# Two-block transformer on one core: the recurrence's order table without zero products, and four steps on other engines

## The chip, the core and the metric

The program runs on one core of a Trainium2 chip. TensorE multiplies matrices, VectorE and GpSimd do elementwise work from and to SBUF (VectorE reads PSUM as well), ScalarE applies activations and scaled copies, SyncE issues the DMAs here. Each engine works through its own list of instructions in order, and waits at semaphores for the others. In the profile's rows they are PE (PEld for the weight loads), DVE, POOL, ACT and SP. The metric is the device time of one execution in microseconds; smaller is better.

## The reference, cut to what matters

The model has a first block (convolution, attention with forgetting, a gated feed-forward) and a second block of two layers, of which the first is a recurrence over 528 positions in 32 heads of 64. Only the recurrence is touched:

```python
kk = (k * k_k); kk = kk / max(norm(kk), 1e-12)         # per head
k = k * (1 + (a - 1) * k_a)
decay = exp(-exp(w))
a_vec, b_vec = -kk, kk * a
def step(S, inp):                                      # S: 64x64 per head
    sa = einsum('bhij,bhj->bhi', S, a_t)
    S = S * w_t + sa * b_t + v_t * k_t
    return S, einsum('bhij,bhj->bhi', S, r_t)
y = (y - mean(y)) * rsqrt(var(y) + GN_EPS)             # per head
y = (y * ln_w + ln_b + bonus) * silu(g)
return y @ w_out
```

## The kernel before

The recurrence is computed in chunks: one of 16 positions and eight of 64. Two heads that fill 128 partitions make a pair, so there are 16 pairs (class `Pair`). For a pair the steps that don't depend on the state are written as generators, cut into pieces by `yield`: `rates` (letter F, decays), `keys` (K, a projection of 48 products of 128x128 by 128x264), `operands` (O), `blocks` (B, small triangular inverses of 16x16, 14 pairs of small products and sums on GpSimd in a row), `inverse` (L) and `merge` (X, the inverses put together to 64x64), `mats` (M, transposes), `weights` (P), `post` (Q, the norm over a head and the gate). `chain` is the recurrence itself: per chunk three steps, each a few small products on TensorE and a move of their result out of PSUM that the next step needs (Z and U on ScalarE, the state S on VectorE).

There is no scheduler: the order of the instructions on every engine is the order in which the code is run. A round starts a new pair's chain (15 of its 27 steps, N) and ends the old pair's (12 steps, O); `MAIN` says in which order the two take turns, and `PLAN` has a word for each of the 27 turns, whose letters say which pieces follow it. A piece that yields 1 leaves its second half (the move out of PSUM) to the next turn or piece. In the same round run the pieces of later pairs: K and F three pairs ahead, O, B and V two ahead, M, X and L one ahead, Q two behind. Rounds -1 to 12 have them all; in the last three the projections and operands have run out and the output projection's pieces stand at K.

The letter D is `fill` (L2175 to 2181): two products with a weight of zeros that add nothing to the sum that `keys` has open. They carry no result. The table has 11 of them in a round.

The names to follow, in the order of `operands`: `sq` (L2032, ScalarE, from `kx`), `kp2` (L2034), `kk` (ScalarE), `n2` (L2043, sums of squares on TensorE), the norms `nv` (L2049, L2050), `mi` (L2055, a mask times the norms), `al` (L2060), `rho` (L2063), `bd` (L2067, L2068, first operands for chunk 0, four small products), `kk2` (L2071), `be` (L2077 and for chunk 0 L2078: beta into `fix_kb`), `ka` (L2080, L2081: kappa into `fix_kb`), then the products `n00` to `n11` (L2101) of `fix_kb` with `AR`, and `n_first` (L2109). The norms' order matters: `kk2` overwrites what `bd` reads. From `n11` and `n_first` the matrix goes to DRAM and back into `n16`, from which `blocks` starts (L2149); at its end it is written out and a transposed copy `t16` of it made (L2158). In `post` the last steps are y (L2389) and the gate (L2391). Which engine does a step says the table `ENG`: a for ScalarE, d for VectorE, p for GpSimd.

Of the kernel before, what the change touches and what calls it, by code (L numbers as in the profile page):

```python
# [1802 lines left out]

PLAN = ("OMOO", "OMOOOKMMD", "OOD", "MLD", "KMQQD", "OPOD", "KPOQKD", "OPOOXQO", "QOKMOKQ", "", "XXKO", "OKQ", "QXKQK", "BXQKK", "MXBQX", "O", "BOMBBXX", "KKQXD", "KBBBD", "BKFD", "XFOQVKFQXQD", "KFQXD", "BXKXFKKK", "FQ", "BMFOKBKQ", "RBBFMB", "KKOXBXKB")

ENG = dict(kx="d", kp2="p", bd="d", ld="p", wc="d", kp="d", kk="a", mi="d", al="d", rho="p", be="d", ka="p", KT="a", vt0="a", vt1="a", KT0="a", VU0="a", y2="a", r2="d", U="a", y0="d", yt="d", no0="p", no1="a", y="d", sg="d", t16="d", Z="a", sc="d", rk="p", kk2="d")  # L1810


def both(new, old):

    for x in MAIN:
        g = new if x == "N" else old
# [3 lines left out]

MAIN = "NONONONONNONONONONNONONONON"


def weave(main, streams):
# [4 lines left out]
    def flush():  # L1831
        while held:
            pull(held.pop())
# [7 lines left out]

    for (i, _), step in zip(enumerate(main), PLAN):
        flush()
# [30 lines left out]
class Pair:  # L1874
# [39 lines left out]
    def ev(s, key, out, x, scale=None, bias=None):  # L1914

        e = ENG[key]
        if e == "a":
# [11 lines left out]
    def en(s, key):  # L1929
        return s.nc.vector if ENG[key] == "d" else s.nc.gpsimd  # L1930

# [94 lines left out]
    def operands(s):  # L2026
# [42 lines left out]
        yield  # L2069
        if ENG["kk2"] == "d":  # L2070
            nc.vector.scalar_tensor_tensor(kk, ta, 1.0, kk, ALU.add, ALU.mult)  # L2071
# [11 lines left out]
        s.rk = T_("rk")  # L2083
        if ENG["rk"] == "d":
            nc.vector.scalar_tensor_tensor(s.rk, rP, k.v("r_k", p), kp, ALU.mult, ALU.mult)
# [198 lines left out]
    def chain(s):  # L2284
# [5 lines left out]
        for c in range(NC_):  # L2290
# [23 lines left out]
            for h, q in enumerate(HS):  # L2314
                mm(z[u, P + 64 * h:P + 64 * h + 64], lhsT=R[u, hw[h]], rhs=Z[u, q], start=h == 0, stop=h == 1)  # L2315
            if ENG["U"] == "d":
                h2 = lambda a: a.rearrange("p (h t) -> p h t", h=2)
# [107 lines left out]
```

## Time and profile before

| | us |
|---|---|
| median of 3 runs (2447.52 to 2453.63) | 2450.68 |
| the profiled execution | 2448.32 |
| its span, first to last instruction | 2446.5 |
| PE busy | 2282.0 (93%) |
| PE weight loads busy | 1964.4 (80%) |
| DVE busy | 1317.8 (54%) |
| POOL busy | 1234.6 (50%) |
| ACT busy | 1001.8 (41%) |

The page of the profile says of busy PE that matmuls are pipelined and their ends modelled: a matmul's row runs from its start to its modelled end, and the next starts before that. How long a product holds TensorE up is read from the start of one row to the start of the next. The idle time that a row shows in brackets is time in which the engine had nothing running, and what ended it; a wait that fits under the tail of the product before is not shown as idle. The recurrence's rounds with all streams lie between 1130 and 1663 us of the span.

### The profile page before, as it was taken

To read this page: it belongs to the slowest core of one execution; us is meant where nothing else is said; L and a number is where in the kernel's file an instruction comes from. 1 tells how busy PE (TensorE), PEld (TensorE's weight loads), DVE (VectorE), ACT (ScalarE), POOL (GpSimd) and SP (SyncE) were. 2 spreads that over 40 slices of the span, in tenths; PEclk is the share of its full clock that TensorE was granted. 3 is DMA by queue.
4 is the path that set the end of the run, shared out by engine and by line. 5 is a ranking of instruction groups with operands and counts; after the bars stand their busy time and mean duration, and the time that the engine had idled before them with its cause. 6 is when DMAs were issued, how large, how long until landed. Compare 5 with 4: busy or idle time off the path is not lost. (4 is left out here: it accounts for less than half of the span.)

```text
span 2446.5 us, 42606 instructions
## 1 busy us (share of the span) xinstructions
PE 2282.0 (93%) x16754; PEld 1964.4 (80%) x16754; DVE 1317.8 (54%) x2860; ACT 1001.8 (41%) x2292; POOL 1234.6 (50%) x1414
## 2 busy tenths in 40 slices
PE   7999999999998999888999999999977898899996
PEld 5788888878887999877888888887877777887885
DVE  6662135734756450323676767676334633765665
ACT  5553333423434442323354444544332422554442
POOL 5235455656655654535456565655333644344433
PEclk9999999999998999998999999997988899999998
DMA  3113222222232423332222323223223332112212
GB/s 130 69 70 122 104 86 87 98 83 104 98 100 86 172 99 126 102 104 85 70 61 55 80 65 74 70 59 103 67 77 110 126 106 101 59 61 64 66 53 96
DMA packets 135496, 217.05 MB, mean 89 GB/s; under 512 B 60864, under 2 KB 85888, under 8 KB 125056
## 3 DMA queue, kind: packets, MB, share of 16 engines
q1 hardware_dynamic: 123168, 191.63, 24.8%
q10 hardware_dynamic: 12128, 22.70, 2.5%
q8 instruction: 132, 2.16, 0.4%
q14 instruction: 68, 0.56, 0.1%
HBM read 179.28 MB, written 35.00 MB: 88 GB/s over the span
## 5 line engine op out<-in xcount | busy, mean ns | idle before, releaser
L261 POOL TENSOR_TENSOR wlo<-wraw,whi 128x512 fp32r<-128x512 f32 (+1 forms) x312 | 440.2, 1440 | 332.8 <-ACT whi L260 332.7
L941 POOL TENSOR_TENSOR wlo<-wraw,whi 128x512 fp32r<-128x512 f32 (+2 forms) x207 | 255.1, 1246 | 320.4 <-ACT whi L940 312.8
L260 ACT ACTIVATE whi<-wraw 128x512 fp32r<-128x512 f32 (+1 forms) x312 | 175.3, 615 | 252.7 <-issue 73.7
L940 ACT ACTIVATE whi<-wraw 128x512 fp32r<-128x512 f32 (+2 forms) x207 | 115.2, 590 | 55.7 <-PE p_o_t L1715 19.4
L269 PE MATMUL pu<-f_xh,whi 128*128 128x512 f32 x336 | 131.2, 391 | 0.0
L271 PE MATMUL pu<-f_xh,wlo 128*128 128x512 f32 x336 | 130.8, 389 | 0.0
L270 PE MATMUL pu<-f_xl,whi 128*128 128x512 f32 x336 | 130.8, 389 | 0.0
L2321 ACT ACTIVATE VU<-z,fix_nv 64x64 f32<-64x64 f32 x256 | 63.2, 301 | 147.0 <-PE z L2315 146.6
L2331 DVE SCALAR_TENSOR_TENSOR fix_S<-fix_S,wc,z 64x64 f32<-64x64 f32 x224 | 62.4, 278 | 93.2 <-PE z L2327 50.2
L1305 POOL COPY ap<-apr 128x96 f32<-128x96 f32 x64 | 16.9, 264 | 141.6 <-DVE apr L1302 102.0
L2154 POOL TENSOR_TENSOR r<-r,t 66x14 f32<-66x14 f32 (+6 forms) x224 | 77.9, 348 | 17.5
L2015 PE MATMUL pk<-lh_k,whi 128*128 128x264 f32 x256 | 81.8, 320 | 1.6 <-DVE kx L1923 1.6
L2015 PE MATMUL pk<-lh_k,wlo 128*128 128x264 f32 x256 | 82.3, 322 | 0.0
L2015 PE MATMUL pk<-ll_k,whi 128*128 128x264 f32 x256 | 79.5, 311 | 0.0
L1601 PE MATMUL p_g<-lh_g,wlo 128*128 128x264 f32 x256 | 73.7, 288 | 2.7 <-POOL wlo L941 2.5
L2152 POOL TENSOR_TENSOR t<-n,r 66x14 f32<-66x14 f32 (+6 forms) x224 | 66.9, 299 | 16.2
L1601 PE MATMUL p_g<-lh_g,whi 128*128 128x264 f32 x256 | 74.8, 292 | 0.0
L269 PEld LDWEIGHTS pu<-f_xh,whi 128*128 128x128 f32 x336 | 63.1, 188 | 13.4 <-issue 0.2
L816 DVE SCALAR_TENSOR_TENSOR ab<-z,vecs,ab 128x511 f32<-128x511 f32 x44 | 55.6, 1265 | 33.7 <-ACT ab L815 33.7
L271 PEld LDWEIGHTS pu<-f_xh,wlo 128*128 128x128 f32 x336 | 63.1, 188 | 13.1
L270 PEld LDWEIGHTS pu<-f_xl,whi 128*128 128x128 f32 x336 | 63.1, 188 | 13.1 <-issue 0.2
L1601 PE MATMUL p_g<-ll_g,whi 128*128 128x264 f32 x256 | 73.1, 286 | 0.0
(850 smaller groups left out, 7508.1 us busy)
## 6 DMA issues: line engine op xcount, KB each, us to landing
wraw<-in_w_up_dram SPq DMA_DIRECT2D x22, 1024.0 KB
wraw<-in_w_dn_dram SPq DMA_DIRECT2D x16, 704.0 KB
wraw<-in_a_h_dram SPq DMA_DIRECT2D x16, 640.0 KB
wraw<-in_l_k_dram SPq DMA_DIRECT2D x16, 576.0 KB
wraw<-in_w_gt_dram SPq DMA_DIRECT2D x8, 1024.0 KB
wraw<-in_l_v_dram SPq DMA_DIRECT2D x8, 1024.0 KB
wraw<-in_l_r_dram SPq DMA_DIRECT2D x8, 1024.0 KB
wraw<-in_l_g_dram SPq DMA_DIRECT2D x16, 512.0 KB
```

The source lines that it names most:

```text
L260: nc.scalar.activation(hi[:p, o], raw[:p, o], AF.Copy)
L261: nc.gpsimd.tensor_tensor(lo[:p, o], raw[:p, o], hi[:p, o].bitcast(F32), ALU.subtract)
L269: nc.tensor.matmul(out, lhsT=wh, rhs=xh, start=start and k == 0, stop=False)
L270: nc.tensor.matmul(out, lhsT=wh, rhs=xl, start=False, stop=False)
L271: nc.tensor.matmul(out, lhsT=wl, rhs=xh, start=False, stop=stop and k == n - 1)
L940: nc.scalar.activation(hi[:, o], raw[:, o], AF.Copy)
L941: nc.gpsimd.tensor_tensor(lo[:, o], raw[:, o], hi[:, o].bitcast(F32), ALU.subtract)
L1601: nc.tensor.matmul(b[:, :HL], lhsT=a, rhs=c[:, o], start=kk == 0 and n == 0, stop=kk == KB - 1 and n == 2)
L2015: s.nc.tensor.matmul(b_[:, :HL], lhsT=a, rhs=b[:, o], start=i == 0 and q == 0, stop=last)
L2152: g.tensor_tensor(tmp[:, :q, :m], n16[:, :q, q:q + 1].to_broadcast([66, q, m]), r16[:, q:q + 1, q + 1:].to_broadcast([66, q, m]), ALU.mult)
L2154: g.tensor_tensor(r16[:, :q, q + 1:], r16[:, :q, q + 1:], tmp[:, :q, :m], ALU.add)
L2321: nc.scalar.activation(VU[u, q], z[u, P + 64 * h:P + 64 * h + 64], AF.Copy, scale=s.nv[u, nv + h:nv + h + 1])
```

## The change

A new `PLAN` and a new `MAIN`. The new table has the same number of letters O, K, B, F, X, Q, P, L, V and R, no D, and two M more (which come after the stream's end and do nothing). In `ENG` four entries change: `bd` and `be` go from VectorE to GpSimd, `y` from VectorE to GpSimd, `t16` from VectorE to ScalarE.

```diff
-PLAN = ("OMOO", "OMOOOKMMD", "OOD", "MLD", "KMQQD", "OPOD", "KPOQKD", "OPOOXQO", "QOKMOKQ", "", "XXKO", "OKQ", "QXKQK", "BXQKK", "MXBQX", "O", "BOMBBXX", "KKQXD", "KBBBD", "BKFD", "XFOQVKFQXQD", "KFQXD", "BXKXFKKK", "FQ", "BMFOKBKQ", "RBBFMB", "KKOXBXKB")
+PLAN = ("OMOO", "OOKMM", "OOOOM", "", "KMLQ", "OQOPOK", "KPM", "QOPOXQ", "QOOKMOKQ", "", "MXXBQKOO", "O", "KKQXQK", "QKKXB", "XBQXM", "", "MXOBKB", "QKXXXK", "MBBB", "BQBFQ", "XFOOBKVKFQX", "FQ", "RKFKQKK", "OF", "BKXKXBK", "FBKKMF", "XXBBOKMBQ")
...
-ENG = dict(kx="d", kp2="p", bd="d", ld="p", wc="d", kp="d", kk="a", mi="d", al="d", rho="p", be="d", ka="p", KT="a", vt0="a", vt1="a", KT0="a", VU0="a", y2="a", r2="d", U="a", y0="d", yt="d", no0="p", no1="a", y="d", sg="d", t16="d", Z="a", sc="d", rk="p", kk2="d")
+ENG = dict(kx="d", kp2="p", bd="p", ld="p", wc="d", kp="d", kk="a", mi="d", al="d", rho="p", be="p", ka="p", KT="a", vt0="a", vt1="a", KT0="a", VU0="a", y2="a", r2="d", U="a", y0="d", yt="d", no0="p", no1="a", y="p", sg="d", t16="a", Z="a", sc="d", rk="p", kk2="d")
...
-MAIN = "NONONONONNONONONONNONONONON"
+MAIN = "NONONONONNONONONONONNONONON"
```

Three places show what moves; all are of round 5, in which chain 5 begins and chain 4 ends. A name's second number is the pair.

TensorE ahead of the operands' products, from the last products of chunk 5 of pair 4's chain on (`pk0_8` is the projection for pair 8). Before:

```order
L2324 MATMUL z5_4_12520<-VU_4_11351,AYb_4_10927 64x64 [waits Activation_49]
L2324 MATMUL z5_4_12520<-VU_4_11351,AYb_4_10927 64x64
L2327 MATMUL z5_4_12520<-VU_4_11351,KTb_4_11350 64x64 x2
L2180 MATMUL pk0_8_12554<-lh_k_7906,fix_zero_7996 128x264 x2
L2306 MATMUL z1_5_12639<-fix_S2_7971,AR_5_11389 128x128 [waits DVE_49]
L2308 MATMUL z1_5_12639<-VU_5_11931,AN_5_11387 64x64 x2
L2015 MATMUL pk0_8_12554<-ll_k_7907,whi108_12052 128x264
L2015 MATMUL pk0_8_12554<-lh_k_7906,wlo108_12053 128x264
L2015 MATMUL pk0_8_12554<-lh_k_7906,whi108_12052 128x264
L2015 MATMUL pk0_8_12554<-ll_k_7907,whi108_12052 128x264
L2180 MATMUL pk0_8_12554<-lh_k_7906,fix_zero_7996 128x264 x2
L2306 MATMUL z6_4_12659<-fix_S1_7970,AR_4_10809 128x128 [waits DVE_49]
```

The same place now, with the first of the operands' products at its end:

```order
L2324 MATMUL z5_4_12388<-VU_4_11263,AYb_4_10849 64x64
L2327 MATMUL z5_4_12388<-VU_4_11263,KTb_4_11262 64x64 x2
L2015 MATMUL pk0_8_12412<-ll_k_7907,whi108_11936 128x264
L2015 MATMUL pk0_8_12412<-lh_k_7906,wlo108_11937 128x264
L2306 MATMUL z1_5_12502<-fix_S2_7971,AR_5_11316 128x128 [waits DVE_49]
L2308 MATMUL z1_5_12502<-VU_5_11821,AN_5_11293 64x64 x2
L2015 MATMUL pk0_8_12412<-lh_k_7906,whi108_11936 128x264
L2015 MATMUL pk0_8_12412<-ll_k_7907,whi108_11936 128x264
L2306 MATMUL z6_4_12513<-fix_S1_7970,AR_4_10758 128x128 [waits DVE_49]
L2308 MATMUL z6_4_12513<-VU_4_11263,AN_4_10735 64x64 x2
L2101 MATMUL n00_7_12524<-AR_7_12432,fix_kb0_7981 128x128 [waits Activation_49,Pool_49]
```

The zero products between the chains' steps are gone, and fewer real ones stand in their place: two between z1 and z6 where four and two zeros stood.

ScalarE at the start of the round, from pair 4's U on. Before:

```order
L2321 ACTIVATE VU_4_11351<-z4_4_12437,fix_nv0_7983 64x64 [waits PE_49]
L2321 ACTIVATE VU_4_11351<-z4_4_12437,fix_nv0_7983 64x64
L1918 ACTIVATE Zb_5_12504<-z0_5_12501 16x128 [waits PE_49]
L2032 ACTIVATE sq_7_12506<-kx_7_11973,vecs_62 128x528 [waits DVE_49,Pool_49]
L1918 ACTIVATE KTa_6_12509<-kt0_6_12512 128x512 [waits PE_49]
L1918 ACTIVATE kk_7_12507<-kx_7_11973,vecs_62 128x528
```

The same place now:

```order
L2321 ACTIVATE VU_4_11263<-z4_4_12307,fix_nv0_7983 64x64 [waits PE_49]
L2321 ACTIVATE VU_4_11263<-z4_4_12307,fix_nv0_7983 64x64
L1918 ACTIVATE t16_6_12074<-r16_6_12073 66x256 [waits DMAHW1_49,DMAHW0_49,Pool_49]
L1918 ACTIVATE Zb_5_12372<-z0_5_12369 16x128 [waits PE_49]
L2032 ACTIVATE sq_7_12374<-kx_7_11853,vecs_62 128x528 [waits DVE_49]
L1918 ACTIVATE KTa_6_12377<-kt0_6_12380 128x512 [waits PE_49]
L1918 ACTIVATE kk_7_12375<-kx_7_11853,vecs_62 128x528
```

The transposed copy, which waits for GpSimd, now stands ahead of everything that ScalarE does for the new round.

GpSimd from the operands' first step to the weights' split. Before:

```order
L2034 TENSOR_TENSOR kp_7_12459<-kp_7_12459,kx_7_11973 128x528 [waits DVE_49]
L2063 TENSOR_TENSOR AR_7_12549<-rP_7_12477,fix_E0_7993 128x4x2x64 [waits DMAHW0_49,PE_49,Activation_49]
L2080 TENSOR_TENSOR fix_kb0_7981<-kp_7_12459,cl_7_12416 128x4x2x64 [waits PE_49,Activation_49,Pool_49]
L2081 TENSOR_TENSOR fix_kb0_7981<-kp_7_12459,cl_7_12416 128x16 [waits PE_49]
L1944 TENSOR_TENSOR wlo109_12633<-wraw109_12479,whi109_12632 128x1152 [waits DMAHW1_49,Activation_49]
L2088 TENSOR_TENSOR rk_7_12650<-rk_7_12650,kp_7_12459 128x528 [waits PE_49,Activation_49]
```

The same place now:

```order
L2034 TENSOR_TENSOR kp_7_12331<-kp_7_12331,kx_7_11853 128x528 [waits DVE_49]
L2063 TENSOR_TENSOR AR_7_12432<-rP_7_12314,fix_E0_7993 128x4x2x64 [waits DMAHW0_49,PE_49,Activation_49]
L2067 TENSOR_TENSOR fix_bd1_7966<-kk_7_12375,fix_E0_7993 64x16 [waits Activation_49]
L2068 TENSOR_TENSOR fix_bd1_7966<-rP_7_12314,fix_E0_7993 64x16
L2067 TENSOR_TENSOR fix_bd1_7966<-kk_7_12375,fix_E0_7993 64x16 [waits Pool_49]
L2068 TENSOR_TENSOR fix_bd1_7966<-rP_7_12314,fix_E0_7993 64x16
L2077 TENSOR_TENSOR fix_kb0_7981<-kk_7_12375,cl_7_12293 128x4x128 [waits DVE_49,PE_49,Pool_49]
L2078 TENSOR_TENSOR fix_kb0_7981<-kk_7_12375,cl_7_12293 128x16 [waits PE_49]
L2080 TENSOR_TENSOR fix_kb0_7981<-kp_7_12331,cl_7_12293 128x4x2x64
L2081 TENSOR_TENSOR fix_kb0_7981<-kp_7_12331,cl_7_12293 128x16
L2088 TENSOR_TENSOR rk_7_12497<-rk_7_12497,kp_7_12331 128x528 [waits Activation_49]
L1944 TENSOR_TENSOR wlo109_12495<-wraw109_12316,whi109_12494 128x1152 [waits DMAHW1_49,Activation_49]
```

Six products more stand ahead of kappa, and the weights' split comes behind `rk` instead of ahead of it.

## Rows read from the trace of the kernel before

**Rows 1.** Windows: us of window, busy per engine, PEclk, DMA share, GB/s.

```profile
0.00:2446.50 2446.50, 2281.97 (x16754) 1964.45 (x16754) 1317.80 (x2860) 1001.78 (x2292) 1234.58 (x1414) 0.96 0.28 89
1194.60:1663.10 468.50, 466.97 (x5672) 390.81 (x5671) 336.00 (x1071) 223.37 (x629) 275.74 (x499) 1.00 0.27 67
1130.00:1163.00 33.00, 21.89 (x149) 19.68 (x148) 18.03 (x32) 9.57 (x19) 18.76 (x36) 0.76 0.20 47
```

**Rows 2.** PE timeline of one round: start, us, engine, line, operation, count.

```profile
1272.14 0.39 PE L2308 MATMUL z<-fix_VU,AN 16*16 16x64 f32 x4
...
1275.86 0.49 PE L2180 MATMUL pk<-lh_k,fix_zero 128*128 128x264 f32 x2
1276.28 0.39 PE L2315 MATMUL z<-Zb,R 16*16 16x64 f32 x4
...
1282.36 0.41 PE L2180 MATMUL pk<-lh_k,fix_zero 128*128 128x264 f32 x2
1282.61 0.39 PE L2306 MATMUL z<-fix_S,AR 128*128 128x128 f32 x2
1282.92 0.44 PE L2308 MATMUL z<-VU,AN 64*64 64x64 f32 x4
1283.30 1.16 PE L2101 MATMUL n<-AR,fix_kb 64*128 64x128 f32 x11
...
1311.25 0.39 PE L2308 MATMUL z<-fix_VU,AN 16*16 16x64 f32 x4
```

**Rows 3.** Windows, the zero products alone: window, busy of PE, PEld, POOL, PEclk.

```profile
1194.60:1663.10 468.50, 61.59 (x264) 41.21 (x264) 0.00 (x0) 1.00 0.27 67
```

**Rows 4.** Waits of PEld, 1194.6 to 1663.1: total us, times, longest us.

```profile
PEld z L2308 <- DVE yt L1923: 2.7, 11, 0.2
PEld z L2306 <- DVE fix_S L2331: 2.5, 12, 0.2
```

**Rows 5.** ACT and DVE timeline, the same round.

```profile
1272.86 0.74 ACT L2032 ACTIVATE sq<-kx,vecs 128x528 f32<-128x528 f32 x1
...
1273.06 1.11 DVE L1923 COPY t<-r 66x256 f32<-66x256 f32 x1
...
1275.51 2.36 DVE L2055 TENSOR_TENSOR AN<-cst_r,fix_nv 128x1152 f32<-128x1152 f32 x1
...
1278.61 0.16 DVE L2067 TENSOR_TENSOR fix_bd<-kk,fix_E 64x16 f32<-64x16 f32 x1
...
1279.16 0.71 DVE L2071 SCALAR_TENSOR_TENSOR kk<-ta,kk 128x528 f32<-128x528 f32 x1
...
1282.17 0.69 DVE L2077 TENSOR_TENSOR fix_kb<-kk,cl 128x512 f32<-128x512 f32 x1
1282.78 0.17 DVE L2078 TENSOR_TENSOR fix_kb<-kk,cl 128x16 f32<-128x16 f32 x1
...
1307.19 0.47 DVE L2389 TENSOR_SCALAR bon<-bon,vecs 128x528 f32<-128x528 f32 x1
```

**Rows 6.** POOL timeline, the same round.

```profile
1275.38 1.28 POOL L2080 TENSOR_TENSOR fix_kb<-kp,cl 128x512 f32<-128x512 f32 x1 [0.24 <-PE kt L2194]
1276.62 1.33 POOL L2081 TENSOR_TENSOR fix_kb<-kp,cl 128x16 f32<-128x16 f32 x1
...
1294.99 0.73 POOL L2149 TENSOR_TENSOR r<-n,cst_r 66x256 f32<-66x256 f32 x1 [0.87 <-DMA vP<-r_vd]
...
1304.22 0.63 POOL L1980 TENSOR_SCALAR sq<-sq 128x528 f32<-128x528 f32 x1 [2.71 <-ACT sq L1979]
...
1310.76 0.21 POOL L2154 TENSOR_TENSOR r<-r,t 66x14 f32<-66x14 f32 x1
1311.74 1.32 POOL L2034 TENSOR_TENSOR kp<-kp,kx 128x528 f32<-128x528 f32 x1 [0.77 <-DVE kx L1923]
```

**Rows 7.** One line or tile, 1194.6 to 1663.1: count, min/median/max ns.

```profile
L2055 DVE TENSOR_TENSOR AN<-cst_r,fix_nv x12: 1358/2352/2360, 1198.6 to 1627.3; 128x1152 f32<-128x1152 f32 x12
L2081 POOL TENSOR_TENSOR fix_kb<-kp,cl x12: 667/1334/1341, 1199.0 to 1628.4; 128x16 f32<-128x16 f32 x12
```

**Rows 8.** Timeline of the first rounds: POOL, DVE and PE.

```profile
1132.06 3.06 POOL L1944 TENSOR_TENSOR wlo<-wraw,whi 128x1152 fp32r<-128x1152 f32 x1 [1.35 <-ACT whi L1941]
...
1133.23 2.44 DVE L2077 TENSOR_TENSOR fix_kb<-kk,cl 128x512 f32<-128x512 f32 x1
...
1135.81 4.23 PE L2101 MATMUL n<-AR,fix_kb 64*128 64x128 f32 x32 [2.95 <-DVE fix_kb L2077]
...
1158.77 3.73 DVE L1923 COPY t<-r 66x256 f32<-66x256 f32 x1 [2.02 <-POOL r L2154]
```

## Prediction

> **What bounds the kernel now.** I read the windows first, then the timeline of one round on each engine, then the waits. Over the span PE is the fullest engine, and between 1194.6 and 1663.1 us it is busy 467.0 of 468.5 us at full clock [rows 1]. That stretch is twelve rounds: the zero products, 22 in a round, stand there 264 times [rows 3]. One round is 39.1 us, from the first product of a new chain at 1272.14 to the next at 1311.25 [rows 2]. The waits of PE in the twelve rounds are small: the two largest groups come to 2.7 and 2.5 us in all, none over 0.2 us [rows 4]. So a round is as long as TensorE's list, and what leaves the list shortens the round, until a wait that the list now covers comes out. DVE is busy 336, ACT 223 and POOL 276 of the 468.5 us [rows 1], so none of them is full; but they are links of a loop, and the loop is what I have to measure against 39.1 us.
>
> **The change part by part.**
>
> *Zero products out.* A pair holds TensorE up from its start to the start of the next row: the first of a round 1276.28 − 1275.86 = 0.42 us, the sixth 1282.61 − 1282.36 = 0.25 us [rows 2]. Read so, the six ahead of `n00` come to 2.4 us and the eleven of a round to 4.1 us. The bounds: at the sixth's price all eleven cost 2.7 us; the busy time of the group gives 61.59 / 12 = 5.1 us [rows 3], but that counts modelled tails. I take 4.1: TensorE's own list is then 35.0 us. A part of the 4.1 may be waiting that the pair covers, since in front of several of them the step behind waits for S or U; that part comes back as a wait, and I count it below.
>
> *beta and the first operands on GpSimd.* On VectorE they cost 4 x 0.16 and 0.69 + 0.17 us [rows 5]. For the large one on GpSimd the nearest row is kappa, of the same shape, 1.28 us [rows 6]. The small ones are not shown free there: the nearest are the smallest product of `blocks`, 0.21 us, and kappa's 16 columns, 1.33 us [rows 6]. The second is so long because it is held: it ends at 1277.95 and VectorE's mask product, which began at 1275.51 and lasted 2.36 us, at 1277.87; that one in turn takes 1.36 us at its fastest and 2.35 at the median [rows 5 to 7], since GpSimd's large kappa ran until 1276.66. So the two engines take turns. I take 0.25 us for each small one (near the free one, as the mask product, the longest that can hold one, comes once in a round), and keep 0.21 and 1.33 as ends.
>
> The Trainium skill says why (SBUF — State Buffer, section SBUF: two separate sides): VectorE with two SBUF inputs and GpSimd take one port pair by an exclusive lock, and the loser waits for the whole instruction. The rows above agree. It speaks against this change: by it all six small products could be held as the 1.33 us one is, which is the second rival below.
>
> *The transposed copy on ScalarE.* 1.11 us leave VectorE [rows 5]. On ScalarE 528 columns of SBUF take 0.74 us [rows 5], so an estimate for 256 is 0.4 us; the strided read is not shown there, so the upper end is VectorE's 1.1. I take 0.4. The edit adds a wait: ScalarE's queue now stands until `blocks` has ended on GpSimd, and behind it are the new chain's first Z, `sq`, `kk` and so all operands.
>
> *The norm's last step on GpSimd.* 0.47 us leave VectorE [rows 5]; on GpSimd the nearest row is another product with scalars over 528 columns, 0.63 us [rows 6]. It stands in the middle of `blocks` and lengthens that by 0.6.
>
> *The loop that this makes.* Time 0 is a round's first product, e the end of `blocks` after it. Today the last small product ends at 1310.97, 0.3 us before the next round begins, and GpSimd idles only 0.77 us ahead of its next step [rows 2, 6]. From e on: the transposed copy 0.4 and the first Z some 0.3; from `sq` to the mask product 2.65 us (1272.86 to 1275.51), the mask product free 1.36; from its end at 1277.87 to the end of `kk2` at 1279.87 2.0, less 0.55 for the `bd` that VectorE no longer does, more 0.3 because `kk2` must wait for `bd` on GpSimd; beta 1.28 + 0.25, kappa 1.28 + 0.25 [rows 5, 6]. That is 9.5, with the semaphores 9.7 us. The products of `n00` can start at e + 9.7.
> TensorE itself comes to `n00` 11.16 us into the round today (1283.30 − 1272.14), so 8.8 without the six pairs [rows 2].
> From `n00` to the start of the next `blocks` 11.7 us pass (1283.30 to 1294.99), most of it through DRAM. `blocks` then runs to 1310.97, 16.0 us, of which 2.7 are a wait for a ScalarE step that hangs on TensorE's list [rows 2, 6]; with the norm's step it needs 13.9 us of GpSimd. The loop from e to the next e is 9.7 + 11.7 + 13.9 = 35.3 us. It is as long as TensorE's new list. So they bind together, and e stays at about 0.2 (the rates' wait that `blocks` sits behind comes 1 us after TensorE's delay). `n00` starts at 9.9 instead of 8.8: a wait of 1.1 us per round. Some of it falls already at the S that z1 and z6 need, which VectorE makes after `kk2`. For the rest of the covered waits (0.2 us each at most today [rows 4]) I take 0.3.
>
> *A round after:* 39.1 − 4.1 + 1.1 + 0.3 = 36.4 us, 2.7 less; twelve rounds 32 us.
>
> *The first rounds* (1130 to 1194.6) wait for the chain of operands and `blocks` rather than for TensorE: 21.9 of 33 us busy [rows 1]. There beta on VectorE took 2.44 us instead of 0.69, behind GpSimd's weight split of 3.06 us, and TensorE waited 2.95 us for it; now beta is queued ahead of the split and ends, by kappa's price, some 1 us earlier. The transposed copy took 3.73 us there, against 1.11 in a full round [rows 5]; on ScalarE GpSimd can't hold it. With a few uncovered zeros I take 4 us off, bounds 0 and 7 [rows 8].
>
> *Begin* (1000 to 1130) and the last three rounds: nothing. Up to 1130 the same steps lie beside the gate's products on TensorE; the last three rounds have no zero products, and their operands are made in the first. If that cover fails, both together cost 3 us either way.
>
> *The sum:* 2448.3 (the profiled execution: 2446.5 of span and 1.8 around it) − 32.4 − 4 = 2411.9 us. The median of the runs is 2.4 above the profiled one, so 2414 us.
>
> **The rivals.**
>
> *The zeros only stood where TensorE waits anyway.* Then each pair taken out is a wait put in: the list gets shorter by 11 pairs, but S and U come no sooner. For it: two equal products cost 0.42 us in the first pair and 0.25 in the sixth [rows 2], so some waiting may be inside the first. Against it: VectorE loses 2.9 us per round, and no engine is nearer to full than 72%. By it a round is 38.8 to 39.1 us and the kernel 2443 to 2451 us: no change.
>
> *GpSimd's small products are held.* Slower, one mechanism: with 1.33 us for each of the six, `bd` takes 5.3 us instead of 1.0. Of the 4.3 more some 1.8 lie beside the mask product, and 2.5 move `kk2`, which must wait for `bd`; the two 16-column products add 2 x 1.08. `n00` can then start only at e + 14.4. TensorE stands 5.8 us in front of it, a round is 35.0 + 5.8 + 0.3 = 41.1 us, 2.0 more than today, and the kernel 2448 + 24 − 4 = 2468, 2470 by the median. It decides from the point where beta and kappa are ready later than 12.6 us into the round (8.8 and the 3.8 that 39.1 − 35.0 − 0.3 leaves). For it: the median of kappa's small product over twelve rounds is 1.33 us [rows 7]. Against it: what holds it is the mask product, and there is one of those per round.
>
> *The clock.* In the twelve rounds it is granted at 1.00, of which 2.4 GHz is the level; in the window from 1130 to 1163, where PE is busy only two thirds, it is 0.76, so partly at 1.2 GHz [rows 1]. A mean of 0.76 over 33 us is 16 us at the lower level. If the new wait at `n00` makes the clock fall for 7 us in each round, under half of that, 3.5 us of work are lost: a round of 39.9, the kernel 2448 + 10 − 4 = 2454, 2456 by the median.
> The Trainium skill has such a case (TensorE: Matmul & The Clock Gate, section A second HAM failure mode: psum-queue depth-cycling): short idle stretches between groups of products, repeated often, made the clock swing. No row of the twelve rounds shows it here, as there is hardly any idle.
>
> **How the numbers follow.** The forecast 0.68, with a range of its own from 2399 (a round of 35.4, first rounds 6 off) to 2438 (38.2, first rounds nothing). The rival without change 0.12, the held products 0.10, the clock 0.10; of this a little goes to faster, since a drop of half that length would still leave a gain. The range for 8 in 10 goes from 2398 to 2453: it takes in no change and leaves out the slower ends. About 0.3%, 7 us, is what a measurement can tell from no change: faster 0.78, within 0.08, slower 0.14.
>
> **What would show it.** Right: the first products of two chains 36 to 37 us apart; no row of L2180; PE idle in front of `n00` of about 1 us, ended by POOL at L2080 or L2081; ScalarE's transposed copy waiting for POOL's last product, under 0.5 us itself; beta on POOL near 1.3 us and the four small products in about a microsecond; PEclk still 1.00. Wrong: PE idle of several microseconds at L2101 (held products), PEclk under 0.95 in the rounds (clock), or waits at L2306 and L2324 that add up to 4 us (the zeros covered waits).

## The result, and the profile after

The changed kernel takes 2417.2 us (median of 4 runs, 2410.9 to 2424.0), the kernel before 2449.1 (2446.8 to 2453.6): a ratio of 0.986, with a 95% interval of 0.984 to 0.988. The profiled execution took 2412.8 us, with a span of 2410.7. One remark on the numbers below: kernels whose clock falls in some rounds scatter by one or two per cent from run to run, and the ratios leave out the longest of those runs; where that matters the lowest and highest time stand beside the median.

Windows of the changed kernel: us of window, busy time per engine, granted clock of TensorE (PEclk), share of DMA, GB/s. They answer to [rows 1].

```profile
...
1199.70:1625.50 425.80, 423.42 (x5408) 351.92 (x5407) 296.68 (x977) 227.63 (x642) 316.92 (x583) 1.00 0.30 73
...
1665.50:1722.10 56.60, 52.58 (x533) 46.09 (x532) 14.98 (x60) 20.18 (x59) 17.68 (x24) 0.89 0.26 81
```

The first row is the twelve full rounds: 425.8 us where there were 468.5 [rows 1], 35.5 a round where there were 39.0. TensorE has 264 products fewer in it (5408 for 5672), which are exactly the zero products of [rows 3], is still busy for 99% of it, and its clock is still granted at 1.00, its level of 2.4 GHz.

The waits of TensorE in those rounds: total us, times, longest us (PE is the products, PEld the weight loads, which answer to [rows 4]).

```profile
PE n L2043 <- ACT sq L2032: 0.7, 1, 0.7
PE z L2308 <- DVE yt L1923: 0.5, 1, 0.5
```

```profile
...
PEld z L2308 <- DVE yt L1923: 3.0, 11, 0.6
...
```

Two real waits in twelve rounds, and none at L2101, where I had put one of 1.1 us in each. One round shows how close it is. Its timeline on PE, DVE, ACT and POOL, for comparison with [rows 2, 5, 6]; time 0 of the round is 1270.48.

```profile
1278.05 0.38 PE L2306 MATMUL z<-fix_S,AR 128*128 128x128 f32 x2
...
1279.81 1.71 PE L2101 MATMUL n<-AR,fix_kb 64*128 64x128 f32 x16
```

```profile
1273.02 0.17 DVE L2049 TENSOR_SCALAR fix_nv<-n 64x10 f32<-64x10 f32 x1 [1.42 <-PE n L2044]
...
1273.87 1.36 DVE L2055 TENSOR_TENSOR AN<-cst_r,fix_nv 128x1152 f32<-128x1152 f32 x1
1275.15 0.71 DVE L2060 TENSOR_TENSOR AR<-kk,fix_E 128x512 f32<-128x512 f32 x1
...
1276.18 0.71 DVE L2071 SCALAR_TENSOR_TENSOR kk<-ta,kk 128x528 f32<-128x528 f32 x1
1276.81 0.45 DVE L2333 COPY fix_S<-z 64x64 f32<-64x64 f32 x2
```

```profile
1270.43 0.64 ACT L1918 ACTIVATE t<-r 66x256 f32<-66x256 f32 x1 [1.00 <-POOL r L2154]
```

```profile
1270.19 0.21 POOL L2154 TENSOR_TENSOR r<-r,t 66x14 f32<-66x14 f32 x1
...
1273.44 0.22 POOL L2067 TENSOR_TENSOR fix_bd<-kk,fix_E 64x16 f32<-64x16 f32 x1
...
1273.91 1.40 POOL L2067 TENSOR_TENSOR fix_bd<-kk,fix_E 64x16 f32<-64x16 f32 x1
1275.28 0.66 POOL L2068 TENSOR_TENSOR fix_bd<-rP,fix_E 64x16 f32<-64x16 f32 x1
1277.05 1.29 POOL L2077 TENSOR_TENSOR fix_kb<-kk,cl 128x512 f32<-128x512 f32 x1 [1.12 <-DVE kk L2071]
...
1278.47 1.29 POOL L2080 TENSOR_TENSOR fix_kb<-kp,cl 128x512 f32<-128x512 f32 x1
...
1300.49 1.71 POOL L2389 TENSOR_SCALAR bon<-bon,vecs 128x528 f32<-128x528 f32 x1
```

Kappa (L2080) ends at 1279.76, and the first score product (L2101), which needs it, starts at 1279.81: GpSimd is ready within a few hundredths of a microsecond of the moment at which TensorE comes. The mask product (L2055) takes 1.36 us where it took 2.36 [rows 5]: kappa used to run beside it, and now stands in GpSimd's queue behind beta, which waits for `kk2` (L2071).

Where the 35.8 us between the two spans come from, by the starts of the same products in both traces: up to 1130 us the changed kernel loses 8.0; from there to the second chain it gains 2.9; twelve rounds gain 42.7; the round after them (40.0 for 42.0) gains 2.0, the next (56.6 for 51.8), the third last, loses 4.8, and the rest gains 1.0.

### The profile page after: what moved, and what is told of

Read it like the earlier page. It is cut to its first block, busy times and chain, and to the rows that moved or that the text cites. A ratio compares the mean times of both kernels' runs of the same rounds, so it can differ in the third digit from the quotient of the medians.

```text
span 2410.7 us, 41987 instructions
## 1 busy us (share of the span) xinstructions
PE 2241.3 (93%) x16446; PEld 1927.8 (80%) x16446; DVE 1257.9 (52%) x2732; ACT 1008.6 (42%) x2308; POOL 1288.3 (53%) x1526
## 5 line engine op out<-in xcount | busy, mean ns | idle before, releaser
L2154 POOL TENSOR_TENSOR r<-r,t 66x14 f32<-66x14 f32 (+6 forms) x224 | 65.3, 292 | 17.5
L269 PE MATMUL pd<-gh,whi 128*128 128x512 f32 x176 | 69.3, 394 | 3.4 <-ACT gh L289 3.4
```

The lines of the kernel that those rows point to most:

```text
L269: nc.tensor.matmul(out, lhsT=wh, rhs=xh, start=start and k == 0, stop=False)
L2154: g.tensor_tensor(r16[:, :q, q + 1:], r16[:, :q, q + 1:], tmp[:, :q, :m], ALU.add)
```

## The experiments

**One part at a time: the zeros, the table, the engines.** Three kernels take the change apart, and a fourth puts the zeros back.

```
e1_zeros_out     before,  PLAN without its letters D
e2_table_only    changed, ENG as before: bd="d", be="d", y="d", t16="d"
e3_engines_only  before,  ENG as changed: bd="p", be="p", y="p", t16="a"
e4_zeros_back    changed, PLAN with the 11 D at the ends of the same turns as before
```

> The kernel before with nothing changed but the zero products taken out: 11 pairs a round leave the old table, all else stays in its turn, and every step is on its old engine. Theory A (a round is TensorE's list, unless the loop through GpSimd's blocks is longer): the list falls to about 35.4 us. In the old arrangement beta ends 11.1 us after the end of blocks, 11.7 pass from there to the next blocks, and blocks itself needs 13.3 without its wait: a loop of 36.1. So a round of 36.1 to 36.4 us, 33 to 36 us off twelve rounds, and no loss in the first rounds: 2412 to 2417 us. Theory B (the zeros stood where TensorE waits anyway, and the gain comes from the new order and the engines): a round of 38.8 or more, 2443 to 2450 us.

> The changed kernel with the four engine moves undone: the new table and the new order of turns, without zeros, with beta, first operands and the norm's step on VectorE and the transposed copy too. Theory A: list 35.4, loop 36.1, so a round of 36.1 to 36.4 us, with beta on VectorE named in front of the score products; the first rounds lose nothing: 2412 to 2417 us. Theory B: the engine moves carry a part of the gain, so that without them a round is 37.5 or more, 2430 us or more. Theory C (the engine moves matter nowhere): a round of 35.4, and the same time as the changed kernel or, if their place in the first rounds cost 5 us there, 2412 us.

> The kernel before with the four engine moves alone: old table, with its zero products, and old turns. Theory A: a round is TensorE's list with the zeros, 39.1 us, so no gain there; the first rounds lose the 5 us that they lost in the changed kernel: 2449 to 2456 us. Theory B: the engine moves carry a part of the gain, a round of 38 or less, 2436 us or less.

> The changed kernel with the zero products put back, the eleven pairs at the ends of the same turns where the old table had them. Theory A: each round pays the list's price for them, 3.6 to 4.1 us, so 39.0 to 39.5 us a round and 43 to 49 us on twelve: 2460 to 2467 us, more than before, since the first rounds keep their loss. Theory B: the zeros stand in waits or make their own price back, a round under 37 us, 2436 us or less.

Measured: zeros out 2553.9 us (2502 to 2557), ratio 1.024 [1.020, 1.028]; table only 2516.4, 1.027 [1.023, 1.031]; engines only 2497.7, 1.018 [1.016, 1.020]; zeros back 2448.5, 0.999 [0.998, 1.000]. Each part by itself makes the kernel slower, by about 2% or more; of these kernels only the one with all three is faster. Of the forecasts only theory B of the table alone (2430 us or more) takes in what was measured, and none had the falling clock that the rows below show. No run has the old order without zeros and with the engine moves, so how much of the gain needs the new order stays open.

Zeros back is the plain one: nine of its rounds, at full clock.

```profile
1237.70:1586.20 348.50, 347.18 (x4258) 292.00 (x4259) 230.84 (x748) 173.89 (x486) 241.42 (x441) 1.00 0.28 70
```

348.5 / 9 = 38.7 us a round against 35.5 without them: 22 zero products cost 3.2 us, inside the prediction's bounds of 2.7 to 5.1 and just under theory A's 3.6 to 4.1, and they hide nothing in this arrangement (the whole time lies between the two theories' ranges). In the old one they hid a wait. In the run with zeros out a round at full clock takes 37.4 us, and in each round TensorE stands for 1.5 us in front of the second block's product with S, which VectorE delivers late (PE timeline, two of its rounds; then two windows, in and behind the second).

```profile
1409.77 0.49 PE L2306 MATMUL z<-fix_S,AR 128*128 128x128 f32 x2 [1.49 <-DVE fix_S L2333]
...
1522.01 0.80 PE L2306 MATMUL z<-fix_S,AR 128*128 128x128 f32 x2 [1.50 <-DVE fix_S L2333]
```

```profile
...
1521.00:1523.00 2.00, 0.99 (x4) 0.77 (x5) 1.93 (x10) 0.00 (x0) 0.00 (x0) 0.74 0.68 168
1523.00:1525.00 2.00, 2.00 (x11) 1.66 (x10) 1.69 (x7) 1.52 (x3) 0.48 (x1) 0.50 0.24 92
```

Five rounds stand that wait at full clock; in the sixth the grant falls to 0.50, 1.2 GHz, inside it, and that round takes 57.5 us and the next 48.4. With the engines alone the wait is another: 1.3 us for the square of the keys on ScalarE, which is queued behind the transposed copy, and that behind the end of `blocks` on GpSimd. Its clock falls in about two of three rounds (44.6 us instead of 40.0). PE, ACT and two windows of one of them:

```profile
1320.13 1.02 PE L2043 MATMUL n<-cst_r,sq 128*64 128x2 f32 x16 [1.31 <-ACT sq L2032]
```

```profile
1318.38 0.64 ACT L1918 ACTIVATE t<-r 66x256 f32<-66x256 f32 x1 [2.17 <-POOL r L2154]
...
1319.34 0.74 ACT L2032 ACTIVATE sq<-kx,vecs 128x528 f32<-128x528 f32 x1
```

```profile
1318.00:1320.00 2.00, 0.82 (x6) 0.56 (x6) 0.12 (x1) 1.57 (x3) 1.92 (x4) 1.00 0.46 115
1320.00:1322.00 2.00, 1.87 (x22) 1.86 (x23) 0.54 (x3) 1.57 (x4) 1.18 (x4) 0.50 0.36 40
```

With the table alone there are two waits in a round, one for S and one in front of the second half of the score products, and in most rounds the clock falls behind one of them (41.4 us, some rounds up to 55). PE of one round, in which it falls at the second:

```profile
1290.82 0.49 PE L2306 MATMUL z<-fix_S,AR 128*128 128x128 f32 x2 [0.50 <-DVE fix_S L2333]
...
1297.35 2.47 PE L2101 MATMUL n<-AR,fix_kb 64*128 64x128 f32 x16 [1.65 <-DVE AYa L2106]
```

**Is it the idle time that lets the clock fall?** If so, work without use in the right place should bring the clock back. Four pairs of zeros, in front of the product that waits:

```
-PLAN = (..., "OPO", ...          (zeros out)
+PLAN = (..., "OPODDDD", ...
```

> The kernel before without its 11 pairs of zero products, as in the first experiment, but with four pairs in one place: right in front of the product with S of the new chain's second block, where that experiment had TensorE idle for 1.5 us in each round. They lie in the wait, 8 x 0.15 to 0.19 = 1.2 to 1.5 us. Theory K (TensorE's idle of 1.5 us makes the granted clock fall, and the fall is what made the kernel without zeros slower than before): the clock stays at 1.00 in the rounds, a round stays at 37.4 to 37.7 us, and twelve rounds give 17 to 20 us: 2428 to 2436 us. Theory W (the clock fell for another reason, such as the smaller work of a round): falls as without zeros, 2490 us or more.

Measured: 2434.4 us (2424.9 to 2436.8), ratio 0.992 [0.990, 0.994], as theory K has it: at least 65 us less than without these eight products a round. Windows of some nine of its rounds, and what is left of the wait there:

```profile
1270.00:1600.00 330.00, 326.12 (x3993) 268.55 (x3994) 251.41 (x807) 165.41 (x463) 205.88 (x366) 1.00 0.29 74
```

```profile
PE z L2306 <- DVE fix_S L2333: 2.9, 9, 0.3
```

The clock is 1.00 and a round 37.4 us: the same length as without zeros at full clock. So the 1.5 us of idle time are the lesser part of that wait's price; what it does to the clock is what made that kernel slower than before.

**Which engine move the new table needs.** Each undone in the changed kernel:

```
e6_copy_back        t16="a" -> t16="d"
e7_beta_back        be="p", bd="p" -> be="d", bd="d"
e8_norm_back        y="p" -> y="d"
e9_beta_only_back   be="p" -> be="d"
e10_first_only_back bd="p" -> bd="d"
```

> The changed kernel with the transposed copy alone back on VectorE. It takes 1.1 us there at the head of the round, ahead of the mask product and of S of the new chain's second block, which ended 0.75 us before TensorE came for it. So TensorE waits 0.3 to 0.5 us there. Theory K (a wait of some tenths of a us in each round is enough for the clock to fall): 2450 to 2520 us. Theory W (only the wait itself counts): a round of 35.8 to 36.0, 2421 to 2425 us.

> The changed kernel with beta and the four first operands back on VectorE. The first operands lengthen VectorE's row in front of S by 0.55 us, which the 0.75 us of spare there just hide; beta follows S on VectorE and ends about 9.5 us into the round, when TensorE comes for the first score product (9.25). Theory K: with a wait of 0.2 to 0.5 us the clock may fall in some rounds: 2425 to 2470 us. Theory W: a round of 35.4 to 35.9, 2417 to 2424 us. The move of the two to GpSimd was worth nothing if the time stays within 2414 to 2420 us.

> The changed kernel with the norm's last step alone back on VectorE. GpSimd's blocks get 1.7 us shorter, so ScalarE's transposed copy and all behind it come earlier; VectorE has 0.5 us more near the round's end. Both theories: the rounds stay at TensorE's list, 35.4 us, and the time within 2412 to 2422 us. If blocks on GpSimd was what set the round, it gets shorter than 35.2 us and the kernel 2410 us or less.

Copy back 2407.4 us, ratio 0.984 [0.981, 0.986]; norm back 2411.6, 0.984 [0.982, 0.987]; beta and first operands back 2532.2 (2512 to 2545), 1.032 [1.028, 1.035]. The first lies under both theories' ranges, the second at the lower end of its own, the third above all of its. The copy's and the norm's place is worth nothing that these runs can tell; the copy lies in VectorE's idle 1.42 us in front of L2049 (above), which I had overlooked. All depends on the third, so I parted it.

> The changed kernel with beta alone back on VectorE; the four first operands stay on GpSimd. Theory L (beta on GpSimd keeps kappa behind it in GpSimd's queue, so kappa no longer runs beside VectorE's row in front of S; with beta away kappa comes right behind the first operands, at 5.9 us into the round, and holds kk2 to its end): kk2 takes 1.7 us instead of 0.7, S of the second block is 1.0 late against a spare of 0.75, TensorE waits 0.3 to 0.5 us, the clock falls in most rounds as it did with both back: 2480 to 2545 us. Theory O (the four small products on VectorE were what made S late with both back, 0.55 us): no wait for S here, a round of 35.4 to 35.9 and 2412 to 2424 us.

> The changed kernel with the four first operands alone back on VectorE; beta stays on GpSimd. Theory L: kappa stays behind beta, nothing of VectorE's row is held, and S comes 0.55 us later, within its spare of 0.75; beta comes 0.5 later too, so TensorE waits 0.4 to 0.5 us at the first score product. If the clock stands it, a round of 35.8 to 36.0 and 2420 to 2426 us, which I take as the likelier; if it falls, 2450 us or more. Theory O: S is late, 2480 to 2545 us.

Beta alone back: 2474.5 us (2459 to 2490), ratio 1.010 [1.006, 1.013]. First operands alone back: 2412.2, 0.984 [0.982, 0.986], with a round of 35.8 as expected (weight loads wait up to 0.5 us at L2101) and a clock of 1.00; both times lie some us under theory L's. So beta is the move that counts in this table. What it does on VectorE, in one round of the run with beta back: DVE, POOL, PE, and two windows.

```profile
1364.33 1.67 DVE L2071 SCALAR_TENSOR_TENSOR kk<-ta,kk 128x528 f32<-128x528 f32 x1
...
1368.57 2.58 DVE L2078 TENSOR_TENSOR fix_kb<-kk,cl 128x16 f32<-128x16 f32 x1
```

```profile
1364.17 1.27 POOL L2080 TENSOR_TENSOR fix_kb<-kp,cl 128x512 f32<-128x512 f32 x1
...
1368.39 2.73 POOL L1944 TENSOR_TENSOR wlo<-wraw,whi 128x1152 fp32r<-128x1152 f32 x1 [0.29 <-ACT whi L1941]
```

```profile
1372.96 3.06 PE L2101 MATMUL n<-AR,fix_kb 64*128 64x128 f32 x16 [1.65 <-DVE AYa L2106]
```

```profile
1370.60:1372.60 2.00, 0.72 (x20) 0.58 (x16) 1.99 (x9) 0.51 (x2) 0.52 (x1) 1.00 0.00 0
1372.60:1374.60 2.00, 1.64 (x11) 1.67 (x12) 1.72 (x8) 0.00 (x0) 0.00 (x0) 0.58 0.00 0
```

Kappa holds `kk2` to 1.67 us, as theory L had it. But S is only 0.3 us late; the wait that decides is a different one. Beta's 16 columns, 0.17 us when free [rows 5], take 2.58: they end at 1371.15, and GpSimd's weight split, which began just ahead of them, at 1371.12. Behind them in VectorE's queue stand the products that read the first scores (L2105, L2106) and so free their banks of PSUM, the memory that TensorE writes to, and TensorE waits 1.65 us for a bank in front of the second half of the scores. The clock falls in it, in nine rounds one after the other: 41.0 us a round. On GpSimd beta stands ahead of the split in the same queue, so the two can't meet. The Trainium skill (SBUF — State Buffer, section SBUF: two separate sides) has the exclusive lock by which the loser waits for a whole instruction; the two ends 0.03 us apart agree with it.

With the first operands back as well, the clock falls in some rounds already at an earlier wait: kappa now holds VectorE's second large product (1.77 us for 0.71), the four small ones follow it, and S is late by half a microsecond. DVE, PE and two windows of one round of that run:

```profile
1294.84 1.77 DVE L2060 TENSOR_TENSOR AR<-kk,fix_E 128x512 f32<-128x512 f32 x1
```

```profile
1298.40 0.49 PE L2306 MATMUL z<-fix_S,AR 128*128 128x128 f32 x2 [0.50 <-DVE fix_S L2333]
1299.94 0.49 PE L2306 MATMUL z<-fix_S,AR 128*128 128x128 f32 x2 [0.24 <-DVE fix_S L2331]
...
1304.94 3.06 PE L2101 MATMUL n<-AR,fix_kb 64*128 64x128 f32 x16 [0.33 <-DVE AYa L2106]
```

```profile
...
1300.00:1302.00 2.00, 2.00 (x18) 1.81 (x19) 2.00 (x2) 0.55 (x2) 1.64 (x1) 0.89 0.00 0
1302.00:1304.00 2.00, 2.00 (x24) 1.78 (x22) 1.99 (x7) 0.00 (x0) 1.09 (x1) 0.50 0.00 0
```

The last test of the clock fills the first of these two waits.

```
 be="d", bd="d", and
-"OQOPOK", "KPM"
+"OQOPOKDD", "KPM"
```

> The changed kernel with beta and the first operands back on VectorE, as in the run of 2532 us, and two pairs of zero products, four in all, right in front of the product that waited 0.50 us for S there. Theory K (that idle half microsecond is what lets the clock fall, and the fall costs the most): the clock stays at or near 1.00, a round is 36.0 to 37.0 us and the kernel 2424 to 2440 us, 90 us less for work that is added. Theory W (the clock falls for another wait or for none): 2490 us or more.

Measured 2491.3 us (2470 to 2528), ratio 1.014 [1.010, 1.019], where it was 1.032: a gain from added work again, but theory W's time, not theory K's: the clock falls for another wait. The expectation rested on the round above, in which the clock was already low when TensorE came to the second half of the scores, and there the wait for the bank was only 0.33 us long. PE of the run with the zeros, one round, and three windows:

```profile
1284.04 2.90 PE L2101 MATMUL n<-AR,fix_kb 64*128 64x128 f32 x16 [1.64 <-DVE AYa L2106]
```

```profile
1281.00:1283.00 2.00, 1.40 (x25) 1.14 (x24) 1.99 (x6) 0.51 (x2) 1.20 (x1) 1.00 0.00 0
1283.00:1285.00 2.00, 0.96 (x6) 0.99 (x7) 2.00 (x9) 0.00 (x0) 0.00 (x0) 0.80 0.00 0
1285.00:1287.00 2.00, 2.00 (x14) 1.78 (x12) 1.17 (x7) 0.00 (x0) 0.00 (x0) 0.50 0.00 0
```

The wait that the zeros cover is gone and the clock passes it at 1.00; it falls later in the round, in or just after the full 1.64 us for the bank, in seven of the nine rounds that have this wait (39.9 to 41.5 us, one of 54.9; the other two take 38.5). Covering one wait hands the fall on to the next.

**A better version.** The copy back on VectorE, and the old table for the last three rounds.

```
+LATE = (the old PLAN)
-weave(both(...), streams)
+weave(both(...), streams, LATE if it >= 14 else PLAN)
```

> A candidate: the changed kernel with the transposed copy on VectorE (no slower in its own run) and with the old table of turns for the pieces of the last three rounds, from the third last on, where the new table put the head's inputs so that TensorE waited 1.97 us in one place and the round took 56.6 us instead of 51.8. If the table is the cause, that round comes back to about 52 us and the time is 2402 to 2409 us at the median, 4 to 5 us under the run with the copy back (2407) or the changed kernel (2417). If that round's length hangs on the clock alone, nothing changes: 2405 to 2418 us.

Measured: 2402.7 us (2398.3 to 2413.8), ratio 0.981 [0.979, 0.983], the lowest of all; the interval lies just under that of the changed kernel and overlaps that of the copy alone. The round in question takes 51.8 us. The longest wait for the head's inputs in it, first in the changed kernel, then here (all line numbers behind the added one are one higher):

```profile
1686.24 0.39 PE L1715 MATMUL p_o_mm<-zh,whi 128*128 128x264 f32 x1 [1.97 <-ACT kp L1734]
```

```profile
1696.16 0.39 PE L1715 MATMUL p_o_mm<-zh,whi 128*128 128x264 f32 x1 [0.84 <-ACT ta L1734]
```

The round before it, still on the new table, took 3.1 us more (43.2 for 40.0), its clock 0.62 for 0.73, so this execution gained less there than the row promises. Nor does the table alone set the round's length: with the engines alone, on the old table, it takes 56.9 us, its clock 0.86 where it was 0.95 before.

## Why the prediction came out right, step by step

2417 against 2414 is right, and the mechanism of the forecast held: TensorE's list sets the round, the zeros were on it, no engine move costs more in this table than it hides. But that the figure comes so close is luck: two errors cancel.

- *Zeros, −4.1 (2.7 to 5.1).* Measured −3.2, with the zeros put back.
- *The loop's wait of 1.1, and 0.3 of other waits.* This is the step that failed in size: there is no such wait. The parts nearly held (beta 1.29 us), but `blocks` ends 0.1 us ahead of the round (1270.40) and not 0.2 behind its start, from there to the first score product it is 9.4 us instead of 9.7, and TensorE comes after 9.3 us instead of 8.8: 0.05 us remain of the 1.1. A round is 35.5 instead of 36.4, twelve gain 42.7 instead of 32.4. Of the 3.6 us that a round lost, 3.2 are the zeros; the rest goes to the new order and the moves as a whole, and no run parts it further. Nor is the path that ends at kappa closed through `blocks` here: with the norm's step back on VectorE (POOL and PE of one round of that run, whose time 0 is 1338.60) `blocks` ends 0.5 us earlier, and the first score product starts after 9.33 us all the same. What kappa waits for begins on TensorE, whose sums of squares end VectorE's idle 1.42 us (L2049, above):

```profile
1337.84 0.21 POOL L2154 TENSOR_TENSOR r<-r,t 66x14 f32<-66x14 f32 x1
...
1347.93 1.71 PE L2101 MATMUL n<-AR,fix_kb 64*128 64x128 f32 x16
```

- *Begin, 0.* Here 8.0 us were lost, and not to the change. The run with the table alone has the begin of before instruction for instruction, and is 7.3 us late at 1130; the run with zeros out, with the same begin, is 0.5 early. One and the same wait at 1009 us lets the clock fall in one execution and not in another (windows of before, then of the table alone):

```profile
1009.00:1012.00 3.00, 1.26 (x9) 1.18 (x10) 2.05 (x7) 0.53 (x1) 0.21 (x2) 1.00 0.16 65
1012.00:1015.00 3.00, 3.00 (x23) 2.74 (x23) 1.45 (x5) 1.65 (x4) 2.71 (x3) 1.00 0.20 75
```

```profile
1009.00:1012.00 3.00, 1.09 (x8) 0.91 (x7) 2.73 (x6) 0.00 (x0) 0.99 (x2) 0.92 0.36 134
1012.00:1015.00 3.00, 3.00 (x15) 2.77 (x14) 0.76 (x2) 1.78 (x3) 1.93 (x2) 0.50 0.24 90
```

- *First rounds, −4.* Measured −2.9. *Last rounds, 0.* Measured +1.8 with the end: 4.8 lost in the third last round, where the forecast thought of the zeros and the operands alone: the new table has the head's products ahead of their inputs, with a wait of 1.97 us and a lower clock behind it.
- *First operands 0.25 us each.* Two did (0.22 and 0.21), two were held, one by VectorE's mask product (1.40) and one by the product behind it (0.66). The second rival was thus half right on the lock, and wrong on its price: VectorE itself is busy with these two products until 1275.86, and `kk2` starts at 1276.18, so the hold can have cost 0.3 us at most.
- *The transposed copy 0.4, the norm's step 0.6.* 0.64 and 1.71, both without effect on the round.
- *"The zeros only stood where TensorE waits".* False of the changed kernel, and true by nearly half of the old arrangement: there 1.5 of 3.2 us come back as a wait for S.
- *The clock, at 0.10 and 2456 us.* It didn't come, but it decides whether the zeros can go: with waits of 0.5 to 1.65 us in a round the clock fell in three of the four partial versions, at a price of 4 to 20 us in that round, where the rival had 3.5. Beta's move was priced as a cost to be hidden; without it the changed kernel is slower than the one before (2474.5 us).
- *Two slips of the sum* change nothing: by its rows VectorE loses 3.1 us a round, not 2.9, and the ends of the forecast's own range, with the 2.4 us of the median, are 2400 and 2440.

## What to carry to other kernels

Before work without use is taken out of the engine that sets the pace, list the waits that it covers, and what each costs with the clock that may fall in it: here zeros out alone was 2% slower, and the whole change 1.4% faster, of which nothing is left when beta alone goes back to its old queue. Two engines that lock each other out are best served by one queue: put the short product ahead of the long one on the same engine rather than beside it. And take a total that fits apart by stages, since a clock that falls in one execution and not in the next can hide an error of the same size.

## What the runs showed of the hardware

- The clock falls in or just after TensorE's waits, but the length of one wait doesn't settle it: waits of 1.5 us went through five rounds at 1.00 and not through the sixth; 1.64 us for a bank went with a fall in seven rounds of nine; 0.50 us for S, with 0.24 us behind, were followed by a fall with beta and the first operands back, and with the table alone passed at full clock in the round shown, while 0.3 us in front of the same product were not followed by one. Which wait is hit stays open. The Trainium skill (TensorE: Matmul & The Clock Gate, section A second HAM failure mode: psum-queue depth-cycling) tells of idle stretches that come again and again and make the clock swing; the runs with beta back show the swing, 1.00 to 0.50 and back in each round.
- A low clock shortens the wait that comes after it (0.33 us where it is 1.64 at full clock), so a round must be read at full clock to see which wait would be next.
- A VectorE product of 16 columns took 0.17 us free and 2.58 beside GpSimd's 2.73 us split: its price is what it meets, not its size.
